# The operand sums of the seven-product scheme built earlier and kept in DRAM, and one more pair in the scheme

## The chip, the cores and the metric

The kernel runs on one core of a Trainium2 chip. The metric is device time in microseconds, start to end of one execution. A core has five engines that run independent instruction queues: PE (matmul; weights are loaded by a second queue, PEld), DVE (vector), ACT (activations), POOL (a second vector engine) and SP, which here only issues DMA transfers. On-chip memory is SBUF (128 partitions) and PSUM, which matmuls write.

## The reference

Two layers over a prompt of 1024 tokens and 8 single-token samples, model width 1024, all in float32. The first layer is gated linear attention with 4 heads (key width 128, value width 256) beside a short convolution:

```python
q, k, v, g, a_low, hb, gate_b, gate_c, z_b = _split(h @ w_in, EVEN_SPLITS)
log_a = jax.nn.log_sigmoid((a_low @ w_gate_up + b_gate_up)) / GATE_TEMP
b = jnp.cumsum(log_a, axis=3)                        # inside a chunk of 64 tokens
qe = q * jnp.exp(b);  ke = k * jnp.exp(-b)
scores = jnp.where(causal, qe @ ke^T, 0.0);  o_intra = scores @ v
ds = (k * jnp.exp(b_last - b))^T @ v;  s = exp(b_last) * s + ds      # chunk by chunk
o = o_intra + qe @ s_prev
o = rmsnorm(o, gla_norm_g) * jax.nn.silu(g)
y, new_buf = causal_dwconv(gate_c * hb, buf, w_sconv)
y = gate_b * y * jax.nn.silu(z_b)
out = jnp.concatenate([o, y], axis=-1) @ w_out
```

The second layer is a longer depthwise convolution between two projections, with a layer norm. `h` is the RMS-normed input of a layer; the kernel multiplies by `norm_g` beforehand (`g0`) and by the root mean square of a token (`rs`) afterwards.

## The kernel before

Activations lie transposed: channels on partitions, the 1032 tokens along the free axis, cut into chunks of 384, 384 and 264 (`CH`). Every float32 operand of a matmul is split into a rounded high part and a residual (`wh`, `wl` for weights; halves of `A` for activations): ACT copies with rounding, and DVE or POOL subtracts. A product of a 128-wide weight block and a chunk is a unit of 24 matmuls: 8 blocks of k, three combinations of the parts (`unit`, line 265).

**Stages.** First the four heads: for each, `kq_proj`, the generator `gla` (the recurrence) and `gates` of the next head run as jobs beside `g_proj` and `v_proj`, which keep PE fed with units. Then 32 blocks of the short convolution's projections in 16 pairs `q`, and the output projection, then the second layer.

**The seven-product scheme.** A pair q in `STRASSEN` (3 to 14) computes two weight blocks against chunks 0 and 1 as a 2x2 block product with seven products of 12 matmuls (`pair_products`, line 707 on) instead of four units of 24; chunk 2 stays plain. Operand sums of the input (four per k: t1, f0, f1, f2) are the same for every pair: `build_t` loads x again (`xa`), scales it on ACT, makes the sums on DVE (`t`, `tf` and a reused `xa`), and splits them into `tq` (ACT copies, POOL or DVE subtracts, lines 704 and 705). It runs as a job beside head 3's end and pair 2. `first_pair` writes t1 over chunk 1 of `A`. The sums of the weights, `s0` and `s1`, are made per pair by `pair_sums`.

**Order.** `start` puts a generator on a list of jobs, with a count of ticks to wait, and `tick`, called after each unit, advances them; a number that a job yields is again a count of ticks. That fixes the order in which instructions are written. ACT runs in the written order. For the other engines a planner orders the instructions when the program is built, with its own costs; each queue then runs strictly in that order, waiting on semaphores.

**Memory.** Nearly all temporary tiles take the next of 25 equal slots (`ring`, line 71), in the order of allocation; a new tile waits until the last reader of the slot's old tile is done, a DMA store among them. PSUM has four slots for units (`mm`) and four for other products (`g`).

**Names.** In `gates`: `tm` and `la` carry the gate's logarithm, `E` the exponentials; PE's three products with `alT` (line 457) start it. In `gla`: `S` is the state before each chunk (DVE lines 555, 557), used by PE at line 581 beside the scores' product at 578; `s` (samples' state), `bc` (decays, keys and queries broadcast from DRAM) and `kv` (outer products, ACT line 564) serve the 8 samples, mostly on POOL (lines 565, 566, 583), and DVE line 584 reduces them; `osq` and `rso` hold the squares of the output `o`, and `sh`, `sl` their split for the column sum (PE line 404).

Of the kernel before, what the change touches and what calls it, by code (L numbers as in the profile page):

```python
# [15 lines left out]
P = 128  # L16
# [33 lines left out]
RMS_AT, RMS_WAIT, GATES_AT = 3, 7, 4  # L50
V_ACT = 2
W_AT = (3, 4)
STAGE_AT, BUILD_AT = (6, 5), 6
STRASSEN = range(3, 15)
EARLY, STAGED = 6, 27
ORDER = "hxw"
GATE_DVE = ((1, 4, 5, 7), (2,), (2, 6))
# [3 lines left out]
def hybrid_step(ctx, tc, xT, wv, wa, wup, woa, wic, woc, par, ident_d, mask_d, smask_d, sgla, ssc, scc,  # L61
# [19 lines left out]
    def T(shape, dt=F32, s="t"):  # L81
        return ring.tile(shape, dt, tag="t", name=nm(s))
# [26 lines left out]
    y_d = dram.tile([KT - 1, 2, P, NT], F32, tag="y_d", name="y_d")  # L109
    x1_d = dram.tile([KT, P, NT], F32, tag="x1_d", name="x1_d")  # L110
    dec_d = dram.tile([H, 3, ND, P], F32, tag="dec_d", name="dec_d")
    wl_d = dram.tile([STAGED, P, KT * P], F32, tag="wl_d", name="wl_d")


# [13 lines left out]
    def start(gen, wait=0):  # L128
        jobs.append([gen, wait])
# [188 lines left out]
    def split_rest():  # L318
        for c, lo, hi in parts_of:
            for k in range(KT):  # L320
                split_x(c, k, xk[k][:, CH[c][0] + lo:CH[c][0] + hi], lo, hi)
                if c and k % 4 == 3:
                    yield
# [128 lines left out]
    def gates(h):  # L452
        la = T([P, NT], s="la")
        tm = T([P, NT], s="tm")
        for lo, n in CH:
            ps = g_t()
            pe.matmul(ps[:, :n], wup_r[:, h * P:(h + 1) * P], alT[:, lo:lo + n], start=True, stop=True)
            act.activation(tm[:, lo:lo + n], ps[:, :n], AF.Abs, bias=pcol("bgu", h))
            dve.tensor_scalar(out=la[:, lo:lo + n], in0=ps[:, :n], scalar1=pcol("bgu", h), scalar2=0.0,
                              op0=ALU.add, op1=ALU.min)  # L460
        tables(LNEXP)
        act.activation(tm, tm, AF.Exp, scale=-1.0)
        tables(LOG)
        act.activation(tm, tm, AF.Ln, bias=1.0)
        dve.tensor_tensor(out=la, in0=la, in1=tm, op=ALU.subtract)
        b = tm
        dve.tensor_tensor_scan(out=b, data0=smask, data1=la, initial=0.0, op0=ALU.mult, op1=ALU.add)
        E1 = T([P, NT], s="E1")
        tables(LNEXP)
        act.activation(E1, b, AF.Exp, scale=1.0 / 16)  # L470
        bv = b[:, :NP].rearrange("p (c l) -> p c l", l=64)
        E3 = la
        dve.tensor_tensor(out=E3[:, :NP].rearrange("p (c l) -> p c l", l=64),
                          in0=bv[:, :, 63:64].to_broadcast([P, 16, 64]), in1=bv, op=ALU.subtract)
        pool.memset(E3[:, NP:], 0.0)
        E2 = b
        act.activation(E2, b, AF.Exp, scale=-1.0 / 16)
        act.activation(E3, E3, AF.Exp, scale=1.0 / 16)
        sm = const.tile([P, 32], F32, tag="sm", name=nm("sm"), bufs=2)
        dve.tensor_copy(sm[:, 0:16], E1[:, :NP].rearrange("p (c l) -> p c l", l=64)[:, :, 63])  # L480
        dve.tensor_copy(sm[:, 16:24], E1[:, NP:])
        smp = sm[:, 0:16].rearrange("p (c t) -> p c t", t=2)
        dve.tensor_tensor(out=sm[:, 24:32], in0=smp[:, :, 0], in1=smp[:, :, 1], op=ALU.mult)
        pool.memset(E1[:, NP:], 1.0)
        pool.tensor_tensor(out=E2, in0=E2, in1=rs2, op=ALU.mult)
        pool.tensor_tensor(out=E3, in0=E3, in1=rs2, op=ALU.mult)
        pool.tensor_tensor(out=E1, in0=E1, in1=rs, op=ALU.mult)
        G[h] = E1, E2, E3, sm
        yield
# [11 lines left out]
    def gla(h, V):  # L501
# [87 lines left out]
        act.activation(rso, o[1], AF.Square)  # L589
        dve.tensor_tensor(out=sq, in0=sq, in1=rso, op=ALU.add)  # L590
        hl = in_parts(sq)
        yield OSQ_WAIT
        for c, (lo, n) in enumerate(CH):
            rstd_chain(colsum_parts(hl, c), rso[:, lo:lo + n], 1.0 / DV, 0)
        for hf in range(2):
            dve.scalar_tensor_tensor(out=o[hf], in0=o[hf], scalar=pcol("gn", hf), in1=rso, op0=ALU.mult, op1=ALU.mult)
            dve.tensor_tensor(out=o[hf], in0=o[hf], in1=SG[h, hf], op=ALU.mult)
        yield 3
        for hf in range(2):
            act.activation(SG[h, hf].bitcast(F32R), o[hf], AF.Copy)  # L600
            (dve if h == H - 1 else pool).tensor_tensor(out=o[hf], in0=o[hf], in1=SG[h, hf], op=ALU.subtract)
# [4 lines left out]
    def g_proj(h):  # L606
        for hf in range(2):
# [4 lines left out]
            act.activation(sg, sg, AF.Silu)  # L612
            SG[h, hf] = sg

    start(split_rest())
    tick()
    start(input_rms(), RMS_AT)
# [3 lines left out]
    for h in range(H):  # L621
        kq_proj(h)
        start(gla(h, Vs[h]))
        if h + 1 < H:
            start(gates(h + 1), HEAD_AT[h])
        g_proj(h)
        if h + 2 < H:
            Vs.append(v_proj(h + 2))
# [44 lines left out]

    TQ, T1 = {}, {}

    def build_t():
        n = CH[0][1]
        xs, fs = [], []  # L680
        t1 = [T([P, 2 * n], s="t1") for _ in range(2)]
        for step in range(6):
            if step < 4:
                xs.append([T([P, 2 * n], s="xa") for _ in range(2)])
                for t, k in zip(xs[step], (step, step + 4)):
                    sp.dma_start(out=t, in_=xT[:, k, 0:2 * n])
            if 0 < step < 5:
                k = step - 1
                a, b = xs[k]
                for t, kk in ((a, k), (b, k + 4)):  # L690
                    act.activation(t, t, AF.Copy, scale=pcol("g0", kk))
                tf = T([P, 2 * n], s="tf")
                f = [tf[:, :n], tf[:, n:], b[:, :n]]
                dve.tensor_tensor(out=f[1], in0=b[:, n:], in1=a[:, n:], op=ALU.subtract)
                T1[k] = t1[k // 2][:, k % 2 * n:k % 2 * n + n]
                dve.tensor_tensor(out=T1[k], in0=a[:, n:], in1=a[:, :n], op=ALU.subtract)
                dve.tensor_tensor(out=f[0], in0=b[:, n:], in1=T1[k], op=ALU.subtract)
                dve.tensor_tensor(out=f[2], in0=b[:, :n], in1=f[0], op=ALU.subtract)
                fs.append(f)
            if step > 1:  # L700
                k = step - 2
                for j in range(3):
                    t = TQ[j + 2, k] = T([P, 2, n], F32R, s="tq")
                    act.activation(t[:, 0, :], fs[k][j], AF.Copy)
                    (dve if k == 3 else pool).tensor_tensor(out=t[:, 1, :], in0=fs[k][j], in1=t[:, 0, :].bitcast(F32),
                                                            op=ALU.subtract)
            yield

    built = build_t()
    start(built, BUILD_AT)  # L710
    def first_pair():
        for k in range(4):
            act.activation(A[1][:, k, :], T1[k], AF.Copy)
            dve.tensor_tensor(out=A[1][:, KT + k, :], in0=T1[k], in1=A[1][:, k, :].bitcast(F32), op=ALU.subtract)

    def put_back():
        lo, n = CH[1]
# [23 lines left out]
    def pair_products(q, take, d0, d1, done):  # L741


        n = CH[0][1]
        e0 = used[0]
        old = put_back() if q == STRASSEN[-1] else iter(())
        next(old, None)
        w0, w1 = W("w0", q, ahead=1), W("w1", q, ahead=0)
        u = T([P, 2, n], s="u2")
        r00, r01 = d0[0][:, d0[1]:d0[1] + n], d0[0][:, d0[1] + n:d0[1] + 2 * n]  # L750
        r10, r11 = d1[0][:, d1[1]:d1[1] + n], d1[0][:, d1[1] + n:d1[1] + 2 * n]
        tq = lambda j: [(TQ[j, k][:, 0, :], TQ[j, k][:, 1, :]) for k in range(4)]
        act.activation(u[:, 0], product(w0, 0, x_quarter(0, 0)), AF.Copy)
        s0 = W("s0", q, ahead=0)
        take(0, 2, unit(2, a_terms(w0, A, 2)))
        add(r00, product(w0, 1, x_quarter(0, 4), g_t), u[:, 0])
        s1 = W("s1", q, ahead=0)
        load_ahead(e0 + 6)
        take(1, 2, unit(2, a_terms(w1, A, 2)))
        p4 = product(w1, 1, tq(4), g_t)  # L760
        if q % 2:
            start(stage_one(q // 2 - STRASSEN[0] // 2))
        split_ahead(e0 + 5)
        add(u[:, 1], product(s0, 1, tq(2)), u[:, 0])
        p5 = product(s0, 0, x_quarter(1, 0), g_t)
        add(r01, p5, u[:, 1])
        next(old, None)
        if q + 1 in STRASSEN:
            pair_sums(q + 1)
        split_ahead(e0 + 6)  # L770
        add(u[:, 0], product(s1, 0, tq(3)), u[:, 1])
        add(r11, p5, u[:, 0])
        add(r10, p4, u[:, 0])
        done(1, slice(0, 2 * n))
        add(r01, product(s1, 1, x_quarter(1, 4)), r01)
        done(0, slice(0, 2 * n))

    def pair_units(q, take, *_):
        for m, j in enumerate(blocks_of(q)):
            i = used[0]  # L780
            left = next((k for k, p in enumerate(plan[i + 1:]) if p[0][0] == "s0"), 9)
            for c, s, ps in units(W("a", j, ahead=min(2, left)), A, (0, 2, 1) if q == 2 * KT - 1 else (0, 1, 2)):
                take(m, c, ps)
                if q + 1 == STRASSEN[0] and m and c == 1:
                    while any(job[0] is built for job in jobs):
                        tick()
                    pair_sums(q + 1)
                    first_pair()

# [575 lines left out]
```

## Time and profile before

| | |
|---|---|
| median of 3 runs | 1279.97 us (1279.8 to 1282.65) |
| profiled execution, its span | 1281.41 us, 1279.6 us |
| TensorE clock granted over the span | 0.996 of full speed |
| PE busy | 1253.8 us, 98% |
| DVE, POOL, ACT busy | 65%, 51%, 45% |

The profiled execution is one of the program's runs with the hardware profiler on. Its span counts from the first to the last instruction. All rows are in microseconds from the start of the span unless they say ns. A wait is put down to the semaphore that came last before the waiting instruction; idle time of an engine that PE does not wait for costs nothing by itself.

### The profile page before, as it was taken

The numbers are of one execution on the slowest core, as the hardware profiler recorded it, in microseconds if no ns is written. First come the engines' busy times: TensorE is split into PE (matmuls) and PEld (weight loads), VectorE is DVE, ScalarE is ACT, GpSimd is POOL, SyncE is SP. The second block draws the span as 40 slices with busy tenths as digits, with TensorE's granted clock in tenths as the row PEclk, the third lists the DMA queues.
The fourth block names the chain that finished last, engine by engine and source line by source line (L and its number), as shares of the span: only waits on it lengthen the run. The fifth ranks groups of instructions, "written<-read, shape, count | busy, mean of one in ns | idle before, by whom it ended". The sixth has DMA issues, their size and how long they took to land.

```text
span 1279.6 us, 20357 instructions
## 1 busy us (share of the span) xinstructions
PE 1253.8 (98%) x8189; PEld 1233.3 (96%) x8189; DVE 828.2 (65%) x1157; ACT 573.6 (45%) x886; POOL 653.2 (51%) x398
## 2 busy tenths in 40 slices
PE   7999999999999999999999999999999999999995
PEld 7999999999999999999999999999999999999995
DVE  5542464345436999999995254314779899978636
ACT  6433525526354543333333143222775839539522
POOL 1455453547374654556546332121298898936410
PEclk9999999999999999999999999999999999999998
DMA  7123042143154323232248998752332223233303
GB/s 243 54 67 137 18 132 104 50 139 130 50 205 149 125 108 116 99 117 93 90 136 308 371 363 330 273 189 95 104 99 94 85 87 104 99 100 132 100 17 133
DMA packets 62495, 174.10 MB, mean 136 GB/s; under 512 B 7729, under 2 KB 25745, under 8 KB 62401
## 3 DMA queue, kind: packets, MB, share of 16 engines
q1 hardware_dynamic: 62112, 172.53, 38.6%
q8 instruction: 64, 1.05, 0.3%
q10 hardware_dynamic: 288, 0.27, 0.1%
q14 instruction: 31, 0.25, 0.1%
HBM read 128.37 MB, written 44.41 MB: 135 GB/s over the span
## 4 chain that ended last, share of the span: by engine, by line
PE 86%; DVE 5%; ACT 3%; DMA 2%; issue 2%; POOL 2%; SPq 1%; DVEq 0%; POOLq 0%; ACTq 0%
PE mm L273 61%; PE mm L734 8%; PE g L734 6%; PE mm L350 4%; PE g L273 1%; PE g L551 1%; PE g L512 1%; PE g L578 1%; PE g L581 1%; PE g L513 1%; PE g L391 1%; DMA xa<-in_dram 1%; POOL wl L243 1%; DMA x<-in_dram 1%; DVE Y L1263 0%
## 5 line engine op out<-in xcount | busy, mean ns | idle before, releaser
L273 PE MATMUL mm<-A,wh 128*128 128x384 f32 (+1 forms) x1536 | 245.5, 311 | 0.0
L273 PEld LDWEIGHTS mm<-A,wh 128*128 128x128 f32 x1536 | 231.3, 188 | 0.8
L243 POOL TENSOR_TENSOR wl<-wr,wh 128x1024 fp32r<-128x1024 f32 x51 | 124.7, 2453 | 190.9 <-ACT wh L239 190.9
L273 PE MATMUL mm<-X,wh 128*128 128x384 f32 (+1 forms) x1152 | 195.6, 320 | 1.2 <-ACT wh L239 0.8
L273 PEld LDWEIGHTS mm<-X,wh 128*128 128x128 f32 x1152 | 182.9, 188 | 4.8 <-DVE X L893 1.4
L239 ACT ACTIVATE wh<-wr 128x1024 fp32r<-128x1024 f32 (+1 forms) x104 | 108.9, 1055 | 140.2 <-PE g L734 51.1
L273 PE MATMUL mm<-A,wl 128*128 128x384 f32 (+1 forms) x768 | 129.6, 310 | 0.0
L273 PEld LDWEIGHTS mm<-A,wl 128*128 128x128 f32 x768 | 117.4, 188 | 0.1
L1027 POOL TENSOR_TENSOR pa<-pa,pr 128x1024 f32<-128x1024 f32 x45 | 110.5, 2456 | 12.8 <-ACT pr L1025 10.4
L350 PE MATMUL mm<-wh,A 128*128 128x256 f32 (+3 forms) x576 | 109.2, 288 | 6.3 <-ACT A L295 6.3
L1013 DVE SCALAR_TENSOR_TENSOR g<-u,late,g 128x512 f32<-128x512 f32 x150 | 102.2, 748 | 1.1 <-ACT g L1010 1.1
L273 PE MATMUL mm<-X,wl 128*128 128x384 f32 (+1 forms) x576 | 102.4, 318 | 0.0
L350 PEld LDWEIGHTS mm<-wh,A 128*128 128x128 f32 (+1 forms) x576 | 87.5, 182 | 8.2 <-ACT A L295 6.3
L273 PEld LDWEIGHTS mm<-X,wl 128*128 128x128 f32 x576 | 92.4, 188 | 0.2
L243 POOL TENSOR_TENSOR wl<-s,wh 128x1024 fp32r<-128x1024 f32 x24 | 67.9, 2839 | 41.1 <-ACT wh L239 41.1
L350 PE MATMUL mm<-wl,A 128*128 128x256 f32 (+3 forms) x288 | 83.0, 289 | 0.5 <-POOL wl L243 0.2
L273 PE MATMUL mm<-M,wh 128*128 128x384 f32 (+1 forms) x384 | 65.0, 320 | 0.0
L273 PEld LDWEIGHTS mm<-M,wh 128*128 128x128 f32 x384 | 61.0, 188 | 0.6
L986 DVE SCALAR_TENSOR_TENSOR g<-us,prm,g 128x512 f32<-128x512 f32 x70 | 52.8, 755 | 12.5 <-ACT g L984 10.9
L200 ACT ACTIVATE ph<-pw 128x1024 fp32r<-128x1024 f32 x27 | 28.6, 1058 | 65.7 <-DMA wl_d<-pw 29.6
L1025 ACT ACTIVATE pr<-u,late 128x512 f32<-128x512 f32 x90 | 57.2, 715 | 0.0
L273 PE MATMUL mm<-b,wh 128*128 128x384 f32 (+1 forms) x336 | 56.5, 319 | 0.0
(286 smaller groups left out, 2498.2 us busy)
## 6 DMA issues: line engine op xcount, KB each, us to landing
wr<-in_dram SPq DMA_DIRECT2D x102, 512.0 KB, 3.4
pw<-in_dram SPq DMA_DIRECT2D x27, 512.0 KB, 6.5
wl_d<-pw SPq DMA_DIRECT2D x27, 512.0 KB, 5.3
wl<-wl_d SPq DMA_DIRECT2D x27, 512.0 KB, 3.6
b<-y_d SPq DMA_DIRECT2D x14, 516.0 KB, 7.4
bc<-dec_d SPq DMA_DIRECT2D x12, 512.0 KB, 5.4
O<-o_d SPq DMA_DIRECT2D x8, 768.0 KB, 10.4
x<-in_dram SPq DMA_DIRECT2D x8, 516.0 KB, 7.3
```

The costliest lines, as they stand in the source:

```text
L200: act.activation(h, r, AF.Copy)
L239: act.activation(h[:, :n], raw[:, :n], AF.Copy)
L243: e.tensor_tensor(out=l[:, :n], in0=raw[:, :n], in1=h[:, :n].bitcast(F32), op=ALU.subtract)
L273: pe.matmul(out, wl if p == "w" else wh, xl if p == "x" else xh, start=((first or into is None) and i == 0), stop=(part[1] and i == len(se ...
L350: pe.matmul(ps[:m, :width], x, y[:, ks], start=(i == 0), stop=(i == 23))
L391: pe.matmul(ps[:, :n], ones, t, start=(i == 0), stop=(i == len(terms) - 1))
L512: pe.matmul(ps[:, j * P:(j + 1) * P], ke[:, lo:lo + P], qe[:, lo:lo + P], start=True, stop=True)
L734: pe.matmul(out, (l if p == "w" else h)[:, ws], xs[k][p == "x"], start=(i == 0), stop=(i == 11))
L986: dve.scalar_tensor_tensor(out=cm if j == 15 else acc, in0=us[:, j:j + n], scalar=ev(j), in1=acc, op0=ALU.mult, op1=ALU.add)
L1013: dve.scalar_tensor_tensor(out=acc[r], in0=u[:, 1 - r, lo + j:hi + j], scalar=df(r, j), in1=acc[r], op0=ALU.mult, op1=ALU.add)
L1025: act.activation(pr[:, r, :], u[:, 1 - r, lo + j:hi + j], AF.Copy, scale=df(r, j))
L1027: pool.tensor_tensor(out=ac, in0=ac, in1=pr, op=ALU.add)
```

## The change

`build_t` moves into the part with the heads. It is started for k = 0 and 1 together with head 1's recurrence and the gates of head 2, and for k = 2 and 3 with head 2's recurrence and the gates of head 3 (`T_AT`). It makes all four sums split (`ts`), with every subtraction on POOL, and stores them in DRAM (`t_d`). Where `build_t` was, `load_t` reads 12 split sums back into `tq`, started after 3 ticks instead of 6, and `first_pair` becomes two loads straight into `A`. The scheme starts at pair 2, so `pair_sums`, the weight splits and seven products are added for that pair, and its plain units for chunks 0 and 1 go. In `gla`, two waits in ticks become shorter for the last head. Line numbers grow by two in the heads (581 becomes 583, 404 becomes 406, 565 becomes 567).

```diff
-STAGE_AT, BUILD_AT = (6, 5), 6
-STRASSEN = range(3, 15)
+STAGE_AT, BUILD_AT = (6, 5), 3
+T_AT = {1: (0, 1), 2: (2, 3)}
+STRASSEN = range(2, 15)
...
+    t_d = dram.tile([4, 4, P, 2, CH[0][1]], F32, tag="t_d", name="t_d")
...
-        yield OSQ_WAIT
+        yield OSQ_WAIT if h < H - 1 else 2
...
-        yield 3
+        yield 3 if h < H - 1 else 1
...
+    def build_t(ks):
+        n = CH[0][1]
+        xa = None
+        for k in list(ks) + [None]:
+            last, xa = xa, None
+            if k is not None:
+                xa = k, [T([P, 2 * n], s="xa") for _ in range(2)]
+                for t, kk in zip(xa[1], (k, k + 4)):
+                    sp.dma_start(out=t, in_=xT[:, kk, 0:2 * n])
+            if last:
+                k, (a, b) = last
+                for t, kk in ((a, k), (b, k + 4)):
+                    act.activation(t, t, AF.Copy, scale=pcol("g0", kk))
+                tf, tg = T([P, 2 * n], s="tf"), T([P, 2 * n], s="tg")
+                t1, f0, f1 = tf[:, :n], tf[:, n:], tg[:, :n]
+                f2 = tg[:, n:]
+                dve.tensor_tensor(out=t1, in0=a[:, n:], in1=a[:, :n], op=ALU.subtract)
+                dve.tensor_tensor(out=f1, in0=b[:, n:], in1=a[:, n:], op=ALU.subtract)
+                dve.tensor_tensor(out=f0, in0=b[:, n:], in1=t1, op=ALU.subtract)
+                dve.tensor_tensor(out=f2, in0=b[:, :n], in1=f0, op=ALU.subtract)
+                yield
+                for j, f in enumerate((t1, f0, f1, f2)):
+                    t = T([P, 2, n], F32R, s="ts")
+                    act.activation(t[:, 0, :], f, AF.Copy)
+                    pool.tensor_tensor(out=t[:, 1, :], in0=f, in1=t[:, 0, :].bitcast(F32), op=ALU.subtract)
+                    sp.dma_start(out=t_d[k, j], in_=t.bitcast(F32))
+            yield
...
         start(gla(h, Vs[h]))
         if h + 1 < H:
             start(gates(h + 1), HEAD_AT[h])
+        if h in T_AT:
+            start(build_t(T_AT[h]))
         g_proj(h)
...
-    def build_t():
...
-    built = build_t()
-    start(built, BUILD_AT)
+    def load_t():
+        for j in (4, 2, 3):
+            for k in range(4):
+                t = TQ[j, k] = T([P, 2, CH[0][1]], F32R, s="tq")
+                sp.dma_start(out=t.bitcast(F32), in_=t_d[k, j - 1])
+            yield
+
+    start(load_t(), BUILD_AT)
+
     def first_pair():
-        for k in range(4):
-            act.activation(A[1][:, k, :], T1[k], AF.Copy)
-            dve.tensor_tensor(out=A[1][:, KT + k, :], in0=T1[k], in1=A[1][:, k, :].bitcast(F32), op=ALU.subtract)
+        for j in range(2):
+            sp.dma_start(out=A[1][:, j * KT:j * KT + 4, :].bitcast(F32), in_=t_d[:, 0, :, j, :].rearrange("k p n -> p k n"))
...
-            start(stage_one(q // 2 - STRASSEN[0] // 2))
+            start(stage_one(q // 2 - 1))
...
-                    while any(job[0] is built for job in jobs):
-                        tick()
```

On POOL, the end of head 1's samples' part stands so before (s are the samples' states, bc the broadcasts, sl the residual of the squares):

```order
L566 TENSOR_TENSOR s_1979<-s_1979,kv_2128 128x1024
L566 TENSOR_TENSOR s_1980<-s_1980,kv_2140 128x1024
L583 TENSOR_TENSOR bc_1975<-s_1979,bc_1977 128x1024
L243 TENSOR_TENSOR wl_2205<-wr_2024,wh_2204 128x1024
L583 TENSOR_TENSOR bc_1975<-s_1980,bc_1977 128x1024
L397 TENSOR_TENSOR sl_2316<-osq_2310,sh_2315 128x1032
```

The same place on POOL in the changed kernel:

```order
L568 TENSOR_TENSOR s_1984<-s_1984,kv_2169 128x1024
L568 TENSOR_TENSOR s_1985<-s_1985,kv_2181 128x1024
L643 TENSOR_TENSOR ts_2193<-tf_2136,ts_2193 128x384
L643 TENSOR_TENSOR ts_2197<-tf_2136,ts_2197 128x384
L585 TENSOR_TENSOR bc_1980<-s_1984,bc_1982 128x1024
L643 TENSOR_TENSOR ts_2201<-tg_2137,ts_2201 128x384
L643 TENSOR_TENSOR ts_2205<-tg_2137,ts_2205 128x384
L245 TENSOR_TENSOR wl_2262<-wr_2057,wh_2261 128x1024
L585 TENSOR_TENSOR bc_1980<-s_1985,bc_1982 128x1024
L399 TENSOR_TENSOR sl_2373<-osq_2367,sh_2372 128x1032
```

Four subtractions of the new `ts` tiles have come between, two ahead of each `bc` product.

On PE, the three gate products of head 2 (g from `alT`, chunks of 384, 384 and 264) stand so before, during head 1's gate projection (mm):

```order
L457 MATMUL g_2068<-alT_176,wup_r 128x384
L457 MATMUL g_2072<-alT_176,wup_r 128x384
L273 MATMUL mm_2101<-A_101,wh_1786 128x384 x16
L273 MATMUL mm_2101<-A_101,wl_1787 128x384 x3
L457 MATMUL g_2076<-alT_176,wup_r 128x264
```

The same products in the changed kernel:

```order
L275 MATMUL mm_2142<-A_102,wh_1787 128x384 x3
L459 MATMUL g_2101<-alT_177,wup_r 128x384
L275 MATMUL mm_2142<-A_102,wh_1787 128x384 x8
L459 MATMUL g_2105<-alT_177,wup_r 128x384
L275 MATMUL mm_2142<-A_102,wh_1787 128x384 x5
L275 MATMUL mm_2142<-A_102,wl_1788 128x384 x8
L275 MATMUL mm_2209<-A_103,wh_1787 128x264 x15
L459 MATMUL g_2109<-alT_177,wup_r 128x264
```

All three have moved back among the matmuls of the units, the third by 5 matmuls of 384 columns and 15 of 264.

On DVE, the recurrence of head 2 (S the state, sg a gate chunk, dq a column copy) stands so before, from the copies of the decays on:

```order
L506 COPY dq_3273<-sm_2847 128x8
L557 SCALAR_TENSOR_TENSOR S_2881<-S_2881,sm_2093,g_2888 128x256
L610 TENSOR_TENSOR sg_2895<-mm_2938,rs_177 128x384
L557 SCALAR_TENSOR_TENSOR S_2881<-S_2881,sm_2093,g_2888 128x256
L557 SCALAR_TENSOR_TENSOR S_2882<-S_2881,sm_2093,g_2928 128x256
L557 SCALAR_TENSOR_TENSOR S_2882<-S_2882,sm_2093,g_2928 128x256
L557 SCALAR_TENSOR_TENSOR S_2882<-S_2882,sm_2093,g_2933 128x256 x2
```

The same place on DVE in the changed kernel (tf, tg the operand sums, xa the scaled input):

```order
L508 COPY dq_3386<-sm_2908 128x8
L635 TENSOR_TENSOR tf_2922<-xa_2824 128x384
L636 TENSOR_TENSOR tg_2923<-xa_2825,xa_2824 128x384
L637 TENSOR_TENSOR tf_2922<-xa_2825,tf_2922 128x384
L557 COPY S_2954<-g_2956 128x256
L638 TENSOR_TENSOR tg_2923<-xa_2825,tf_2922 128x384
L559 SCALAR_TENSOR_TENSOR S_2954<-S_2954,sm_2126,g_2956 128x256
L559 SCALAR_TENSOR_TENSOR S_2954<-S_2954,sm_2126,g_2961 128x256 x2
```

The four sums stand ahead of and inside the first half of S, which stood ahead of these decay copies before; the second half of S comes behind six other instructions, with the next four sums between its steps.

## Rows read from the trace of the kernel before

**Rows 1.** The page's first part: busy time, share, instructions.

```profile
PE 1253.8 (98%) x8189; PEld 1233.3 (96%) x8189; DVE 828.2 (65%) x1157; ACT 573.6 (45%) x886; POOL 653.2 (51%) x398
```

**Rows 2.** Waits of PE: instruction, releaser, us in total, times, longest.

```profile
...
PE g L734 <- DVE wl L243: 1.4, 1, 1.4
...
PE g L404 <- ACT sh L396: 1.0, 1, 1.0
...
PE g L734 <- ACT wh L239: 0.7, 1, 0.7
```

**Rows 3.** Timeline at the stage's entry: start, us, engine; then idle time and releaser.

```profile
433.67 1.66 PE L734 MATMUL g<-A,wh 128*128 128x384 f32 x8 [0.69 <-ACT wh L239]
...
431.31 0.94 ACT L704 ACTIVATE tq<-tf 128x384 fp32r<-128x384 f32 x2 [1.44 <-DVE tf L697]
```

**Rows 4.** Timeline of POOL, 217 to 246 us (head 1).

```profile
225.90 4.76 POOL L566 TENSOR_TENSOR s<-s,kv 128x1024 f32<-128x1024 f32 x2
230.63 2.39 POOL L583 TENSOR_TENSOR bc<-s,bc 128x1024 f32<-128x1024 f32 x1
...
235.34 2.39 POOL L583 TENSOR_TENSOR bc<-s,bc 128x1024 f32<-128x1024 f32 x1
242.59 2.41 POOL L397 TENSOR_TENSOR sl<-osq,sh 128x1032 fp32r<-128x1032 f32 x1 [4.86 <-ACT sh L396]
```

**Rows 5.** Timeline of ACT in the same stretch.

```profile
220.33 4.78 ACT L564 ACTIVATE kv<-bc,vT 128x128 f32<-128x128 f32 x16
...
241.45 1.06 ACT L396 ACTIVATE sh<-osq 128x1032 fp32r<-128x1032 f32 x1 [1.30 <-DVE osq L590]
```

**Rows 6.** Timeline of PE at a product of 12 matmuls.

```profile
452.48 1.56 PE L734 MATMUL g<-tq,wh 128*128 128x384 f32 x8
453.88 0.86 PE L734 MATMUL g<-tq,wl 128*128 128x384 f32 x4
```

**Rows 7.** DMA issues, 160 to 460 us: count, KB each, median us to landing.

```profile
xa<-in_dram SPq DMA_DIRECT2D x8, 384.0 KB, 6.1
```

**Rows 8.** Timeline of PE and ACT around the third gate product of head 2.

```profile
208.88 2.09 PE L273 MATMUL mm<-A,wh 128*128 128x264 f32 x16
210.81 1.14 PE L273 MATMUL mm<-A,wl 128*128 128x264 f32 x8
...
208.21 0.48 ACT L458 ACTIVATE tm<-g,prm 128x264 f32<-128x264 f32 x1 [2.50 <-PE g L457]
```

**Rows 9.** Instructions on tile tq: duration ns min/median/max, starts.

```profile
L705 POOL TENSOR_TENSOR tq<-tf,tq x6: 1019/1330/4359, 414.4 to 428.2; 128x384 fp32r<-128x384 f32 x6
```

**Rows 10.** Instructions on tile xa, in the same form.

```profile
L691 ACT ACTIVATE xa<-xa,prm x8: 920/938/964, 406.6 to 422.6; 128x768 f32<-128x768 f32 x8
```

**Rows 11.** Timeline of ACT, POOL, DVE and PE in head 2.

```profile
301.04 1.07 ACT L478 ACTIVATE la<-la 128x1032 f32<-128x1032 f32 x1 [3.54 <-POOL E L484]
...
305.72 2.41 POOL L486 TENSOR_TENSOR la<-la,rs 128x1032 f32<-128x1032 f32 x1
...
296.26 0.42 DVE L555 COPY S<-g 128x256 f32<-128x256 f32 x1
...
301.84 2.53 DVE L557 SCALAR_TENSOR_TENSOR S<-S,sm,g 128x256 f32<-128x256 f32 x5
...
302.14 0.60 PE L578 MATMUL g<-scT,V 128*128 128x128 f32 x4
```

**Rows 12.** Timeline of DVE, 412 to 428 us: the sums as built before.

```profile
413.15 0.55 DVE L697 TENSOR_TENSOR tf<-xa,t 128x384 f32<-128x384 f32 x1
...
424.80 1.25 DVE L697 TENSOR_TENSOR tf<-xa,t 128x384 f32<-128x384 f32 x1
```

**Rows 13.** Timeline of DVE and POOL: one small sum in heads 1 and 2.

```profile
218.43 0.17 DVE L483 TENSOR_TENSOR sm<-sm 128x8 f32<-128x8 f32 x1
...
295.79 5.17 POOL L565 TENSOR_TENSOR s<-s,bc 128x1024 f32<-128x1024 f32 x2 [15.67 <-DMA s<-in_dram]
...
299.01 1.98 DVE L483 TENSOR_TENSOR sm<-sm 128x8 f32<-128x8 f32 x1
```

More of the change, by code (lines that the diff above doesn't have):

```diff
@@ L671, in conv_state @@
         dve.tensor_scalar(out=cf[:, :, 1, 0:1], in0=ev[:, :, 0:1], scalar1=-1.0, scalar2=None, op0=ALU.mult)
-    TQ, T1 = {}, {}
-    def build_t():
[L679 to L706, printed above, removed]
@@ L707, in build_t @@
+    TQ = {}
+    def load_t():
[3 more added lines that the diff above has]
+                sp.dma_start(out=t.bitcast(F32), in_=t_d[k, j - 1])
             yield
-    built = build_t()
-    start(built, BUILD_AT)
+    start(load_t(), BUILD_AT)
     def first_pair():
-        for k in range(4):
-            act.activation(A[1][:, k, :], T1[k], AF.Copy)
-            dve.tensor_tensor(out=A[1][:, KT + k, :], in0=T1[k], in1=A[1][:, k, :].bitcast(F32), op=ALU.subtract)
+        for j in range(2):
+            sp.dma_start(out=A[1][:, j * KT:j * KT + 4, :].bitcast(F32), in_=t_d[:, 0, :, j, :].rearrange("k p n -> p k n"))
```

## The prediction

> **What bounds the kernel now.** I read the page's first part and the waits of PE for the whole span first. PE is busy for 1253.8 of 1279.6 us [rows 1], so a gain must take matmuls or a wait away from PE, and a loss is anything that makes PE wait once more. The waits of PE are few: apart from the start and the final norms, two stand at the entry to the seven-product stage (1.4 and 0.7 us, line 734) and one, 1.0 us, at line 404, the column sum over head 1's output squares [rows 2]. Then I read the timelines of the other engines around these places, and around every place where the new work lands. For the entry the reader is to see that PE waits at 433.67 us for a `wh` of ACT, and that ACT at 431.31 is still at its copies of the operand sums, waiting for DVE's `tf` [rows 3]: the old building of the sums is what makes the two entry waits. For line 404 he is to see that PE waits at the end of a chain that has no gap: POOL runs from 225.90 to 237.73 us back to back, and reduction, square, sum and copy follow on DVE and ACT until 242.51, when PE starts [rows 4, 5]. Whatever is put on POOL in that stretch comes out at PE one to one.
>
> **What the change takes away.** Eight matmuls of a product take 1.40 us (452.48 to 453.88), 0.175 each, a product of 12 takes 2.10 [rows 6]. A pair of two plain blocks has 2 x 2 units of 24 such matmuls that the scheme replaces by seven products of 12: 96 against 84. The third pair joining removes 12 matmuls, 2.1 us. The two entry waits, 2.1 us together [rows 2], lose their cause, because the copies and differences of the sums leave ACT and DVE there. Twelve loads and two more take their place, on SP's queue and the DMA engines, with the wait of the fourth product for them some 10 us behind the entry. A load of the same size lands a median 6.1 us after issue [rows 7] and in the changed program's order the twelve stand ahead of the raw weights of the first pair, behind nothing but free slots of the ring; I count that as covered. If the cover is gone, the entry waits are back in another form (a rival below). So the gain is 4.2 us; between 2.1 (entry waits stay) and 4.6 (each wait also gives back the start of a matmul stream, some 0.2 us).
>
> **What it adds in head 1.** The sums of k = 0 and 1 are made beside the gates of head 2, while head 1's recurrence runs. Three edits meet here.
> First, PE's third gate matmul for head 2 (line 457, 264 columns) stood behind 16 and 3 matmuls of a unit. In the changed order it stands behind that whole unit and 15 matmuls of the next. That is 5 x 0.175 and 15 x 0.12 (1.93 us for 16 matmuls of 264 columns, 208.88 to 210.81) = 2.7 us later [rows 8]. ACT's Abs waits for that matmul and starts at 208.21, and from it runs the chain of exponentials, scan, differences and gate products up to POOL's state update at 225.90. In it I find no idle time that anything outside the chain ends, so 2.7 us pass through.
> Second, POOL gets four residual splits of 128x384 between the state updates and the second `bc` product. In the old place such a split took 1.02 us at least and 1.33 in the median [rows 9]. Four are 4.1 to 5.3 us; with DVE quiet there I take 1.02, 4.1 us. They stand ahead of `bc`, and what is queued behind them on POOL is just that, `wl`, and the second `bc`, for which DVE's reduction and at last PE's column sum wait.
> Third, four adds on DVE and two scalings on ACT come ahead of the outer products `kv`, 2 x 0.94 us on ACT [rows 10]. POOL takes `kv` up at 225.90, though ACT begins its 16 pieces at 220.33 and has the first eight, half of 4.78 us, by 222.7 [rows 5], so 1.9 us are hidden there behind POOL's three gate products. DVE's next copy of V waits for POOL in the changed order, since V now gets the slot of a `kv` tile; PE will therefore stop once before the column sum, in the next V unit, but on the same clock, and the sum is not changed by it.
> Head 1 together: 2.7 + 4.1 = 6.8 us; at least 4.1 (if the first is absorbed somewhere), at most 8.0 with 1.33 a split.
>
> **What it adds in head 2.** Here the order interleaves the adds with the recurrence of S itself, for which the inter-block matmuls (line 581) wait. Before, PE was there at 302.14 us, and S was made from 296.26 on. Now PE does one unit more ahead of it, 24 x 0.175 = 4.2 us, and would come at 306.3. The scalings stand on ACT behind the exponential of `la`, which ends at 302.11 us because POOL's memset releases it [rows 11]; with 0.94 each they end at 303.05 and 303.99. Then DVE does three adds, the copy to S (0.42), a fourth add and the first step of S (0.5, five in 2.53 us) [rows 11]. An add took 0.55 us beside an idle POOL and 1.25 beside a busy one [rows 12], and POOL is busy until 308.13 [rows 11]. With 1.25: 303.05 + 4 x 1.25 + 0.42 + 0.5 = 308.97, 2.6 us after PE. With 0.55, and the second add waiting for its operand: 303.99 + 3 x 0.55 + 0.42 + 0.5 = 306.56, 0.2 us. I take the busy value. The second half repeats it: four adds between four steps of S, 4 x 1.25 + 4 x 0.5 = 7.0 us, beside one unit and two thirds of a short one on PE, 4.2 + 1.9 = 6.1. That is 0.9 us of waiting, 1.0 with the operands a little late; nothing with 0.55. Head 2: 3.6 us, between 0.2 and the 5.7 worked out next.
> One row speaks for more. A sum of 8 columns took 1.98 us at 299.01 and ended with POOL's running product, at 300.96; the same form took 0.17 us at 218.43 [rows 13]. If each add waits until the running POOL product ends, and POOL's next waits for the add, the first three adds start at 303.4, 306.3 and 309.2, the copy, the fourth add and S's first step end at 311.3, 5.0 us after PE, and with 0.7 in the second half head 2 costs 5.7.
> The Trainium skill, page "SBUF — State Buffer", section "Who interferes with whom", states this as a rule: an instruction of VectorE with two SBUF inputs contends with a GpSimd instruction that reads SBUF, and who starts first holds the shared pair for its whole length. The 8-column sum agrees with it; the adds of 1.25 us stood beside short products of POOL, so that they do not tell the two apart. By the rule the sum below would be 2.1 us more.
>
> **The sum.** -4.2 + 6.8 + 3.6 = +6.2 us. The profiled execution took 1281.4 us, so it would be 1287.6; the median of the runs is 1280.0, and on that clock I predict 1286.2. PE has no slack later on in which to win back a wait, since it is the bound everywhere.
>
> **Rivals.**
> Blocked adds (above): head 2 costs 5.7, the sum is +8.3 and the time 1288.3. For it the row of 1.98 us; against it that POOL had only memsets queued behind that product, so that the row does not show the two taking turns. Chance 0.2.
> Late operands at the entry: the two loads for the first pair's first operands stand on SP behind stores that wait for head 3's output, and the twelve others move 4.7 MB. If the fifth product waits as long as one such load takes to land, 6.1 us [rows 7] come on top: 1292.3. For it, the entry is dense on SP; against it, the new code lets head 3's column sum wait two ticks instead of four. Chance 0.1.
> Only POOL's splits count: the gate chain absorbs its 2.7 us, head 2 runs with adds of 0.55. Then -4.2 + 4.1 + 0.2 = 0.1, and the time is 1280. For it, ACT and DVE are idle for half of this stretch; against it, the chain without gaps in rows 4 and 5. Chance 0.18.
> The other side: no wait in the heads, so faster. The mechanism is that POOL's splits fall into POOL's idle stretches, of which there is one of 4.86 us before 242.59 [rows 4], and not ahead of `bc`. Place: line 404's column sum. It decides if POOL reaches the second `bc` no later than at 237.7 us as before; then only the gain is left, -4.2 us, 1275.8. Against it stands POOL's queue, which is in order, with the splits ahead. Chance 0.12.
>
> **How the numbers follow.** The forecast itself has 0.4; its own range is 1281 to 1289.5 (head 1 from 4.1 to 8.0, head 2 from 0.2 to 5.7, not all at one end). A measurement of this kernel tells about 0.3% from no change, 3.8 us: below 1276.1 is faster, above 1283.8 slower. Slower: 0.2 + 0.1 and 0.32 of the forecast's 0.4, 0.62. Same: 0.08 of the forecast, 0.15 of the third rival, 0.01 of the last, 0.24. Faster: 0.11 of the last and 0.03 of the third, 0.14. The range of 1277 to 1292 leaves out most of the last rival and the worst of late operands.
>
> **What would show it.** In the changed profile: the row of line 734 waiting at the entry gone; PE's waits grown by one for `sh` (now line 406) of some 3 us and one in a V unit before it, together near 7; POOL's `ts` splits at 1.0 to 1.3 us directly ahead of `bc` in head 1; a wait of PE's line 580 or 583 for S in head 2 of 2 to 5 us; `tf` and `tg` adds of 1.25 us there. The prediction is wrong if the column sum of head 1 does not come later against the start of that head's recurrence, if S in head 2 is ready at PE's arrival, or if the entry has a new wait for `tq` or `A`.

## The result, and the profile after

The changed kernel took 1289.83 us in the median of six runs (1289.61 to 1292.81), the kernel before beside it 1281.64 (1279.80 to 1282.74). The ratio over the runs is 1.0075, 95% interval 1.0065 to 1.0085; the two medians alone stand at 1.0064. In a second session, with the kernel before at 1280.48, it took 1290.93, ratio 1.0082 (1.0068 to 1.0096). It is slower by 0.6 to 0.8%: the predicted direction, in the predicted range, 3.6 us above the predicted 1286.2.

The profiled execution took 1291.6 us with a span of 1289.8, 10.2 us more than before. The page's first part answers to [rows 1]: twelve matmuls fewer, but PE is busy 2 us longer.

```profile
PE 1255.9 (97%) x8177; PEld 1235.7 (96%) x8177; DVE 813.6 (63%) x1161; ACT 576.8 (45%) x889; POOL 658.4 (51%) x405
```

The waits of PE over the whole span answer to [rows 2]: us in total, times, longest.

```profile
PE mm L352 <- DVE V L355: 4.9, 1, 4.9
PE g L580 <- DVE S L559: 4.4, 1, 4.4
PE g L406 <- ACT sh L398: 2.1, 1, 2.1
```

The two rows of the entry are gone. From 420 to 470 us PE was busy for 47.95 us before; now it is for all 50 (first number after the length; then PEld, DVE, ACT, POOL, the granted clock, the DMA share).

```profile
420.00:470.00 50.00, 50.00 (x327) 50.00 (x326) 39.37 (x45) 17.27 (x19) 20.96 (x11) 1.00 0.43 149
```

In head 1, PE reaches the third gate product of head 2 and the column sum later. First two lines: before; last two: changed.

```profile
207.88 0.29 PE L457 MATMUL g<-alT,wup_r 80*128 80x264 f32 x1
242.57 0.74 PE L404 MATMUL g<-sh,ones 128*128 128x384 f32 x3 [0.96 <-ACT sh L396]
210.13 0.29 PE L459 MATMUL g<-alT,wup_r 80*128 80x264 f32 x1
249.93 0.73 PE L406 MATMUL g<-sh,ones 128*128 128x384 f32 x3 [2.12 <-ACT sh L398]
```

POOL's timeline answers to [rows 4].

```profile
221.06 2.43 POOL L489 TENSOR_TENSOR E<-E,rs 128x1032 f32<-128x1032 f32 x1
...
225.81 2.75 POOL L488 TENSOR_TENSOR la<-la,rs 128x1032 f32<-128x1032 f32 x1
228.53 5.29 POOL L568 TENSOR_TENSOR s<-s,kv 128x1024 f32<-128x1024 f32 x2
233.78 2.28 POOL L643 TENSOR_TENSOR ts<-tf,ts 128x384 fp32r<-128x384 f32 x2
236.02 2.38 POOL L585 TENSOR_TENSOR bc<-s,bc 128x1024 f32<-128x1024 f32 x1
238.36 1.99 POOL L643 TENSOR_TENSOR ts<-tg,ts 128x384 fp32r<-128x384 f32 x2
...
242.68 2.38 POOL L585 TENSOR_TENSOR bc<-s,bc 128x1024 f32<-128x1024 f32 x1
```

The reader is to see the four splits (two rows of two) between the state update and the second `bc`, with no gap, and the state update at 5.29 us where it took 4.76. DVE's timeline runs beside it: four adds, each as long as one of POOL's products, and behind them the copies of V, for which PE waits 4.9 us. They begin as the adds end and 0.3 us after POOL's state update (233.82); e3 and e8 come back to which of the two holds them.

```profile
223.80 2.48 DVE L635 TENSOR_TENSOR tf<-xa 128x384 f32<-128x384 f32 x1 [2.87 <-ACT xa L631]
...
231.65 2.58 DVE L638 TENSOR_TENSOR tg<-xa,tf 128x384 f32<-128x384 f32 x1
234.15 1.40 DVE L355 COPY V<-mm 128x256 f32<-128x256 f32 x4
```

In head 2, DVE, POOL and PE answer to [rows 11]:

```profile
310.36 0.88 DVE L635 TENSOR_TENSOR tf<-xa 128x384 f32<-128x384 f32 x1 [1.89 <-ACT xa L631]
311.19 2.73 DVE L636 TENSOR_TENSOR tg<-xa,xa 128x384 f32<-128x384 f32 x1
313.85 2.70 DVE L637 TENSOR_TENSOR tf<-xa,tf 128x384 f32<-128x384 f32 x1
...
324.99 0.55 DVE L636 TENSOR_TENSOR tg<-xa,xa 128x384 f32<-128x384 f32 x1
...
310.79 2.72 POOL L489 TENSOR_TENSOR E<-E,rs 128x1032 f32<-128x1032 f32 x1
313.46 2.67 POOL L488 TENSOR_TENSOR la<-la,rs 128x1032 f32<-128x1032 f32 x1
...
318.27 1.22 PE L580 MATMUL g<-scT,V 128*128 128x128 f32 x4 [4.43 <-DVE S L559]
```

Each long add begins shortly after a product of POOL began and ends just after it, and these products take 2.7 us instead of 2.4 themselves: the two engines take turns. With POOL idle (324.99) the same add takes 0.55 us. PE stops for 4.43 us, and its first four matmuls then take 1.22 us, against 0.60 in [rows 11]. The windows of two microseconds show the granted clock in that stretch (PE busy, then the clock):

```profile
318.00:320.00 2.00, 1.73 (x8) 0.50 0.73 290
320.00:322.00 2.00, 2.00 (x11) 0.50 1.03 410
322.00:324.00 2.00, 2.00 (x14) 0.57 0.25 94
324.00:326.00 2.00, 2.00 (x14) 1.00 0.37 121
```

0.50 is the lower of the two levels, 1.2 GHz. The 28 matmuls of lines 580 and 583 up to the next projection unit took 5.72 us (318.27 to 323.99); before, they took 3.04 us (302.14 to 305.18, clock 1.00). The unit behind them, before and changed:

```profile
305.18 3.05 PE L273 MATMUL mm<-A,wh 128*128 128x384 f32 x16
323.99 3.05 PE L275 MATMUL mm<-A,wh 128*128 128x384 f32 x16
```

So the wait costs 4.43 us and another 2.7 behind it.

### The profile page after: what moved, and what is told of

It is laid out like the page before. It is cut to its first block, busy times and chain, and to the rows that moved or that the text cites. A ratio compares the mean times of both kernels' runs of the same rounds, so it can differ in the third digit from the quotient of the medians.

```text
span 1289.8 us, 20425 instructions
## 1 busy us (share of the span) xinstructions
PE 1255.9 (97%) x8177; PEld 1235.7 (96%) x8177; DVE 813.6 (63%) x1161; ACT 576.8 (45%) x889; POOL 658.4 (51%) x405
## 4 chain that ended last, share of the span: by engine, by line
PE 74%; DVE 5%; ACT 2%; issue 1%; POOL 1%; DVEq 0%; ACTq 0%; POOLq 0%
PE mm L275 54%; PE mm L743 8%; PE g L743 6%; PE g L275 1%; PE g L580 1%; PE g L583 1%; DVE cv L1171 1%; PE g L393 1%; DVE Y L1270 0%; PE g L514 0%; DVE sqv L1157 0%; DVE tm L469 0%; DVE x L897 0%; POOL ts L643 0%; PE g L515 0%
## 5 line engine op out<-in xcount | busy, mean ns | idle before, releaser
L275 PE MATMUL mm<-A,wh 128*128 128x384 f32 (+1 forms) x1472 | 234.8, 310 | 0.0
L275 PEld LDWEIGHTS mm<-A,wh 128*128 128x128 f32 x1472 | 220.6, 188 | 0.9
L245 POOL TENSOR_TENSOR wl<-wr,wh 128x1024 fp32r<-128x1024 f32 x49 | 120.9, 2474 | 183.4 <-ACT wh L241 183.4
L275 PE MATMUL mm<-A,wl 128*128 128x384 f32 (+1 forms) x736 | 123.2, 308 | 0.0
L275 PEld LDWEIGHTS mm<-A,wl 128*128 128x128 f32 x736 | 111.8, 188 | 0.1
```

The source lines that it names most:

```text
L245: e.tensor_tensor(out=l[:, :n], in0=raw[:, :n], in1=h[:, :n].bitcast(F32), op=ALU.subtract)
L275: pe.matmul(out, wl if p == "w" else wh, xl if p == "x" else xh, start=((first or into is None) and i == 0), stop=(part[1] and i == len(se ...
```

## The experiments

All edits are to the changed kernel. Two theories were held. Turn-taking: the adds on DVE alternate with POOL's long products, and that makes the wait in head 2. Queue: the splits on POOL stand ahead of `bc`, and that makes the wait for `sh` in head 1. A third question is whether the slow matmuls come from the wait.

**Without the third pair (e1).**
```diff
-STRASSEN = range(2, 15)
+STRASSEN = range(3, 15)
```


> The changed kernel with the scheme from pair 3 on again, the early sums kept. Theory: the third pair is worth its 12 matmuls, 2.1 us, and nothing else, since its entry shows no wait; so 1289.8 + 2.1 = 1291.9 us, the waits of PE in heads 1 and 2 as they are. Rival (a later start of the scheme gives the operands of the first pair time, or the third pair costs as much on the other engines as it saves): 1289.8 or less.

Measured 1294.23 us (1293.36 to 1294.72), ratio 1.0103 (1.0088 to 1.0118), span 1292.3. The waits of 4.9, 4.4 and 2.2 us stand as they were. The span is 2.2 to 2.5 us above the two profiles of the changed kernel, of which 0.6 is a longer wait at the start; the medians differ by 3.3 and 4.4, and 1294.23 is 2.3 above the expected 1291.9. The spans agree with a pair worth its twelve matmuls, 2.1 us; the medians leave room for more, which is not shown.

**One more tick behind S in head 2 (e2).**
```diff
-            yield
+            yield 1 if Q and h == 2 else 0
```


> The changed kernel with one more tick in head 2 between the recurrence of S and the products that read it, so that PE has one more unit of 24 matmuls (4.2 us) ahead of them. Theory: PE's 4.4 us at line 580 shrink to some 0.2 to 0.5, and with the wait goes the stretch at granted clock 0.5 behind it, which lengthened the 36 matmuls of lines 580 and 583 from 3.0 to 5.7 us; so 4.2 + 2.7 = 6.9 us less, 1282.9. Rival 1 (the clock falls for another reason than the wait): 4.2 less, 1285.6. Rival 2 (S is late against whatever PE does, as it follows the unit): no change, 1289.8.

Measured 1290.27 us (1289.88 to 1292.23), ratio 1.0076 (1.0061 to 1.0091). The wait for S stayed at 4.4 us, and PE's order in head 2 did not change, so the edit did not put the unit where it was meant to go; that the planner's due times set the order there is not shown. The run says nothing on either theory. (The matmuls behind the wait are 28, not the 36 of the expectation.)

**The gate projections one place earlier (e3).**
```diff
-HEAD_AT = (6, 3, 1)
+HEAD_AT = (6, 2, 1)
```


> The changed kernel with the gates of head 2 started one tick earlier (2 instead of 3), so that PE's third gate matmul comes some 6 us earlier. Theory: the chain from ACT's Abs to the column sum of head 1 moves up until DVE's S steps, which wait for POOL's fourth split, hold it: some 3.5 us; the column sum at 246.4 instead of 249.9, 1286.3. Rival (the gate matmul's place does not matter, since POOL's splits alone delay the sum): column sum at 249.9, 1289.8.

Measured 1294.73 us (1293.70 to 1294.78), ratio 1.0106 (1.0091 to 1.0121), span 1293.0: worse, and expected otherwise. The wait of PE in head 1, and two lines of DVE's timeline there:

```profile
PE mm L352 <- DVE sg L612: 9.8, 1, 9.8
```

```profile
225.18 1.36 DVE L612 TENSOR_TENSOR sg<-mm,rs 128x384 f32<-128x384 f32 x3 [10.54 <-DMA t_d<-ts]
...
236.56 0.42 DVE L355 COPY V<-mm 128x256 f32<-128x256 f32 x1 [4.59 <-POOL s L568]
```

POOL reached its gate products 6 us earlier (E at 214.76 instead of 221.06), but two rows of splits now stood directly behind them, ahead of the state update, which started at 231.64 behind ACT's `kv`, 3.1 us later than without the edit. PE waits for DVE's gate chunk `sg`, and DVE stood idle ahead of it for 10.54 us, until the store of a split (`t_d<-ts`) was done. So the wait moved to another place and grew. The second line shows one thing more: the adds were over at 231.97, and the copy of V still waited for POOL's state update.

**The sums later in both heads (e4, e5, e9).**
```diff
+T_WAIT = {1: 8, 2: 6}
-            start(build_t(T_AT[h]))
+            start(build_t(T_AT[h]), T_WAIT[h])
```


> The changed kernel with the building of the sums started 8 ticks later in head 1 and 6 in head 2, so that POOL's splits stand behind the second bc product and the adds behind the steps of S. Theory: both losses, 7.4 us in head 1 and 7.1 in head 2 (4.4 of waiting, 2.7 of clock), go and the gain of 4.2 stays: 1289.8 - 14.5 = 1275.3, plus up to 2.4 where the residual's column sum now stands directly behind the first: 1275 to 1278, below the kernel before. Rival (the same work on POOL, ACT and DVE has to collide somewhere; the waits of PE come back at the gates or at the entry): 1283 or more.

Measured 1281.55 us (1279.91 to 1283.36), ratio 1.0006 (0.9996 to 1.0016), above the expected 1275 to 1278 and below the rival's 1283. The two large waits are gone; the waits of PE between 200 and 470 us are

```profile
PE g L407 <- POOL sl L400: 1.7, 1, 1.7
PE g L407 <- ACT sh L399: 1.0, 1, 1.0
PE mm L353 <- DVE V L356: 0.7, 1, 0.7
```

all between 241.1 and 246.2 us, and the granted clock falls behind them:

```profile
244.00:248.00 4.00, 2.76 (x12) 0.61 0.11 47
248.00:252.00 4.00, 4.00 (x20) 0.54 0.87 346
```

The 1.0 us is the wait of before [rows 2]. The 1.7 comes from the order: the residual part of the column sum now follows the main part directly, where 36 matmuls stood between before.

With ten places in head 1 (`T_WAIT = {1: 10, 2: 6}`):

> The building of the sums started 10 ticks later in head 1 and 6 in head 2 (8 and 6 in the run before). With 10 the residual's column sum stands again behind the small V unit and 12 matmuls, as in the kernel before. Theory: the three short waits that stood close together in the run before (1.0, 1.7 and 0.7 us) shrink to the 1.0 of the kernel before, the granted clock stays at 1.0 there, and only the gain is left: 1289.8 - 14.5 = 1275.3 us, 4 to 5 below the kernel before. Rival (the later work delays the weight splits behind it on POOL, or the clock falls as before): 1279 to 1282.

Measured 1282.89 us (1282.15 to 1285.96), ratio 1.0022 (1.0013 to 1.0031): the rival, and 0.9 above its range. The residual no longer waits, but the sums' copies on ACT stand ahead of the weight split, and PE waits for it:

```profile
PE mm L276 <- ACT wh L242: 4.2, 1, 4.2
```

Behind it the granted clock falls, to 0.91 in the mean of 260 to 300 us.

With nine (`T_WAIT = {1: 9, 2: 6}`):

> The sums of head 1 start nine places later instead of eight (e4: 1281.6, e5 with ten: 1282.9), and those of head 2 six places later as there. In the order of instructions the residual part of head 1's column sum then stands behind 24 + 8 matmuls of projections instead of directly behind the main part, as it did in the kernel before, while the splits of the weights are not yet pushed back as with ten places. Theory: the waits of e4 in head 1 (1.7 us for the residual, 1.0 for the main part, 0.7 for V) shrink to the 1.0 of the kernel before, the clock then stays at full speed, and the whole gain of 4.2 us stays: span near 1275.5, time 1276 to 1277, ratio 0.997. Rival: the later sums run into the weight splits of the next stage as with ten places: a wait for wh of some 4 us around 240 to 270 us, time 1280 to 1283, ratio 1.000 to 1.002.

Measured 1276.28 us (1275.69 to 1277.02), ratio 0.9968 (0.9956 to 0.9981): faster than both kernels, as expected; span 1274.2. Between 200 and 430 us PE waits only

```profile
PE g L407 <- ACT sh L399: 1.0, 1, 1.0
PE mm L276 <- ACT wh L242: 0.4, 1, 0.4
```

and the windows have the clock at full speed in both heads (last but two).

```profile
210.00:260.00 50.00, 48.60 (x377) 47.46 (x377) 27.43 (x45) 33.64 (x57) 31.08 (x20) 1.00 0.31 121
...
300.00:360.00 60.00, 60.00 (x395) 57.96 (x395) 40.33 (x58) 34.74 (x59) 45.41 (x32) 1.00 0.43 158
```

The turns are still there: an add beside POOL's `bc` takes as long as that product.

```profile
314.98 2.63 DVE L637 TENSOR_TENSOR tg<-xa,xa 128x384 f32<-128x384 f32 x1
...
314.50 2.70 POOL L586 TENSOR_TENSOR bc<-s,bc 128x1024 f32<-128x1024 f32 x1
```

But S was complete by then (its last steps began at 301.20), so that nobody waits. What costs is not the blocked add but what is queued behind it.

**Only head 2's sums later (e6).** `T_WAIT = {1: 0, 2: 6}`

> The changed kernel with the building started 6 ticks later in head 2 alone; head 1 as it is. Theory: the wait of 4.4 us at line 580 and the 2.7 us of slower clock behind it go, the waits of head 1 (4.9 and 2.1) stay: 1289.8 - 7.1 = 1282.7. Rival (the clock's part is not head 2's): 1289.8 - 4.4 = 1285.4.

Measured 1285.30 us (1284.73 to 1285.69), ratio 1.0037 (1.0023 to 1.0051), span 1283.7. The wait for S is gone and the clock is 1.00 from 300 to 360 us, with PE busy throughout; head 1 keeps its waits, the one for `sh` at 2.2 us, the one for V at

```profile
PE mm L353 <- DVE V L356: 4.9, 1, 4.9
```

The span is 6.1 and 6.4 us below the two of the changed kernel, the median 4.5 and 5.6 below. The theory had 7.1 (wait and slow matmuls), the rival 4.4 (the wait alone). The medians do not decide between them. In the profiles the second comparison is the fairer one, since both have a fall of the clock behind the later wait of head 1 (e10 below): 4.4 of wait and 2.0 more. So in these two profiles the slow matmuls go with the wait, at a lower price than 2.7.

**POOL's products beside the adds left out (e7).**
```diff
-        pool.tensor_tensor(out=E2, in0=E2, in1=rs2, op=ALU.mult)
+        if h != 3:
+            pool.tensor_tensor(out=E2, in0=E2, in1=rs2, op=ALU.mult)
```
(the two products that follow, likewise)

> The changed kernel without POOL's three products of the last head's gates (they leave the factor rs out of E, tm and la of that head), so that POOL is idle while DVE does the first four adds in head 2; the adds keep their place ahead of S. Theory (an add of DVE waits until POOL's running product ends): the adds take 0.55 to 1.0 us instead of up to 2.7, PE's wait at line 580 falls from 4.4 to 0.6 or less, the clock stays up, and the time is 1289.8 - 7 = 1282.8. Rival (S is late because of the adds' place and ACT's scalings alone): the adds keep their times or the wait stays at 2.5 or more, 1287 or more.

Measured 1285.78 us (1284.53 to 1287.37), ratio 1.0042 (1.0028 to 1.0056), span 1284.9. The same add in the same place, and PE's wait for S:

```profile
312.61 0.56 DVE L637 TENSOR_TENSOR tg<-xa,xa 128x384 f32<-128x384 f32 x1 [0.27 <-ACT xa L632]
```

```profile
PE g L581 <- DVE S L560: 0.6, 1, 0.6
```

0.56 us instead of 2.73, and 0.6 of waiting instead of 4.4, with the clock at 1.00: turn-taking is shown to be the cause in head 2. The waits of head 1 stay (5.0 and 2.3 us). The time is 3 us above the 1282.8 that the theory gave. The span is 4.9 below the first profile of the changed kernel and 5.2 below that of e10, which, like this one, has the clock down to 0.94 from 200 to 260 us; e10's own terms, 3.8 us less waiting and 1.6 of slow matmuls, make 5.4. The Trainium skill, page "SBUF — State Buffer", section "Who interferes with whom", says that a VectorE instruction with two SBUF inputs contends with a GpSimd instruction that reads SBUF; this run agrees, with 0.56 against 2.73 us.

**Head 1 without POOL's splits (e8).**
```diff
+                    if ks[0]:
                         pool.tensor_tensor(out=t[:, 1, :], in0=f, ...)
+                    else:
+                        act.activation(t[:, 1, :], f, AF.Copy)
```


> The changed kernel without POOL's residual splits for k = 0 and 1 (ACT writes a second copy in their place; the residuals are left out). Theory: the column sum of head 1 is ready 4.3 us earlier, but the wait for DVE's copy of V before it (4.9 us), which is set by POOL's state update ahead of the splits, stays; so PE arrives at the column sum at 247.8 instead of 249.9 and gains only 2.1: 1287.7. Rival (the splits are all of head 1's loss beyond the gates): 4.3 less, 1285.5.

Measured 1288.98 us (1288.57 to 1290.02), ratio 1.0069 (1.0053 to 1.0084), span 1286.8.

```profile
PE mm L352 <- DVE V L355: 5.4, 1, 5.4
```

The wait for `sh` is gone and the one for V stays, so the splits on POOL make the first and not the second. What makes the second, the run does not tell: the fourth add and POOL's state update end 0.4 us apart here (233.35 and 232.94) as in the changed kernel (234.23 and 233.82). The line of e3 shows that POOL's state update holds the copy of V even when the adds are long over, as the prediction had it; what the adds alone would cost there is not shown. The time fell by 0.9 and 2.0 us against the two medians of the changed kernel; 2.1 was expected.

**The changed kernel again (e10).**

> The changed kernel itself, unedited, beside the run above and the same runs of the kernel before, so that the edits can be set against it on one chip. Expected 1289.8, ratio 1.0075, waits of 4.9, 4.4 and 2.1 us in heads 1 and 2 and the granted clock near 0.5 behind the 4.4. If the waits or the clock vary from run to run, the prices taken from single profiles (2.7 us for the clock in head 2) would have to be read with that scatter.

Measured 1290.93 us (1289.58 to 1292.15). The waits are the same to 0.1 us, the clock is not:

```profile
252.00:254.00 2.00, 2.00 (x12) 0.50 0.00 0
...
320.00:322.00 2.00, 2.00 (x11) 0.50 0.87 340
322.00:324.00 2.00, 2.00 (x16) 0.78 0.93 375
```

Behind the wait of 2.2 us in head 1 the clock fell too, which it had not done in the first profile, and behind the 4.4 in head 2 it rose sooner: that group took 4.67 us (319.65 to 324.32), 1.6 more than at full speed instead of 2.7. The span differs by 0.3 us only.

The link between wait and clock in head 2 holds over all twelve profiles:

| kernel | wait for S in head 2, us | clock, 300 to 360 us |
|---|---|---|
| changed, e1, e2, e3, e8, e10 | 4.4 (e2: another 0.4) | 0.94, 0.97, 0.97, 0.94, 0.94, 0.97 |
| before, e4, e6, e9 | none | 1.00 |
| e5, e7 | 0.8 (two of 0.4), 0.6 | 1.00 |

## Why the prediction was right, and where its size was off

**The gain, -4.2 us: held.** No wait at the entry, no new one for `tq` or `A`; e1 gives the third pair at 1.6 to 2.5 in the spans, without and with the longer wait at the start. e9, which has the change without its large new waits, lies 4.2 us below the kernel before in the medians (5.4 in the spans). The rival of late operands had no part.

**Head 1, +6.8: 7.4 measured (249.93 against 242.57).** The gate matmul came 2.25 us later (210.13 against 207.88), not 2.7. The four splits took 4.27, and 4.2 counted from start to start, against 4.1. A term was missing: the adds slow POOL's own products, `la` and the state update, by 0.9 us. I had taken DVE as quiet there. The wait in the V unit that the prediction named is the 4.9, with the releaser that it named (e3), and the two waits make 7.0 together, "near 7". The clock fell behind the first of them, to 0.70 from 236 to 240 us, and that was absorbed, because PE then came later to the second, which POOL's chain sets. e9 bears out that the gate matmul's place passes through: there it came at 206.52, 1.36 us earlier than before, and the column sum at 241.23, 1.34 earlier. But in the changed kernel PE's order is not all that holds this chain. ACT's pieces for the first two gate products waited for the store of a split, and the third piece began only 0.16 us after them:

```profile
209.24 1.05 ACT L460 ACTIVATE tm<-g,prm 128x384 f32<-128x384 f32 x2 [4.30 <-DMA t_d<-ts]
210.45 0.48 ACT L460 ACTIVATE tm<-g,prm 128x264 f32<-128x264 f32 x1 [0.16 <-PE g L459]
```

By these lines, an earlier third matmul with all else in its place would have gained no more than that. The prediction has no such wait; e9 took both away.

**Head 2, +3.6: 7.1 measured. This is the step that failed, in its size.** The prediction put an add at 1.25 us; two of the first three took 2.7, as the rival of blocked adds had it (5.0 us of waiting worked out, 4.43 measured). The evidence was in [rows 13], and plainer still 4 us ahead of the second line of [rows 12]. The add of 1.25 stands beside splits of 1.3 us; this one stands beside a long product of POOL:

```profile
420.65 2.83 DVE L694 TENSOR_TENSOR tf<-xa,xa 128x384 f32<-128x384 f32 x1 [1.52 <-ACT xa L691]
420.66 2.40 POOL L243 TENSOR_TENSOR wl<-wr,wh 128x1024 fp32r<-128x1024 f32 x1
```

e7 settles it. For the second half the prediction had 1.0, the rival 0.7; PE did not wait there, because POOL was idle from 324.20 to 325.83 us and three of the four adds took 0.55. The fourth, beside POOL again, took 2.37. The other 2.7 us (1.6 in e10) are in no case of the prediction: they are the clock behind the wait. Without them head 2 is 4.4 and the sum 7.6, 1.4 above the forecast's 6.2.

With the gain as predicted and the two heads as measured, the sum is -4.2 + 7.4 + 7.1 = 10.3, and the spans differ by 10.2. PE's totals split this into 8.1 us more idle and 2.1 more busy. The forecast's own range ended at 1289.5; that 1289.8 lies in the stated one is owed to its room up to 1292, which also had the late operands in view, and they had no part. The rival of blocked adds, at 1288.3, was nearer than the forecast.

**The other rivals.** "Only POOL's splits" needed adds of 0.55 and an absorbed gate chain; neither came. The side without waits needed POOL to be done with the second `bc` by 237.7 us (the prediction says "reaches"; before, POOL began it at 235.34 and ended at 237.73); here it began at 242.68. e9 shows that this side can be had: the same work, nine and six places later, took 1276.3 us, near that rival's 1275.8.

## What to carry to other kernels

Work that fits into an engine's idle share must still be placed behind that engine's critical chain in its queue, not ahead of it: the same change costs 0.6 to 0.8% or gains 0.3% by the place of the sums alone. Where DVE and POOL both stream from SBUF, count an added DVE instruction at the length of the POOL product that it meets (here 2.7 us against 0.55), and count what it does to POOL as well (2.7 against 2.4). To a wait like the 4.4 us here add the slower matmuls that follow (1.6 to 2.7 us), unless a later wait absorbs them.

## What the runs showed of the hardware

The granted clock went to the 1.2 GHz level behind a single wait of 4.4 us (a price of 1.6 to 2.7 us), behind three short ones of 1.0, 1.7 and 0.7 us close together (e4), and behind one of 2.2 us in one profile (e10) while the same kernel's 2.1 us left it at 1.00 in another. Before, the entry's 0.7 and 1.4 us left it at 1.00. The Trainium skill, page "TensorE: Matmul & The Clock Gate", section "What's actually happening", says of a kernel's first matmuls that how many of them run at the lower level differs from run to run of the same kernel; the two profiles here show the like behind a wait in its middle.

A copy on DVE with one input took longer beside POOL too: in the changed kernel's head 2, beside the state product, one of 128x16 took 2.37 us, in head 1 with POOL not busy 0.17. No run takes POOL's product away to show the cause.

```profile
220.47 0.17 DVE L482 COPY sm<-E 128x16 f32<-128x16 f32 x1
...
303.66 2.37 DVE L482 COPY sm<-E 128x16 f32<-128x16 f32 x1
```
